# A hybrid decoder step on one Trainium2 core: the RWKV-7 recurrence's small products on the whole TensorE array, its outputs in groups of four chunks

## The chip, the cores and the metric

The kernel runs on one core of a Trainium2 chip. Five engines run side by side, each in its own fixed order: TensorE (PE, with its weight loads PEld), VectorE (DVE), ScalarE (ACT), GpSimd (POOL) and SyncE (SP, which here issues nearly all DMAs). The metric is the device time of one launch in microseconds (us), as the median of several runs.

## What is computed

One layer takes 2048 prompt tokens and 64 sample tokens (8 sequences of 8 with a paged cache of 1024 positions). After an RMSNorm one projection feeds two groups of eight heads of width 64: stick-breaking attention, and RWKV-7 time mixing. Both outputs are gated, concatenated, projected and normed. The part that the change is about is the recurrence of the second group:

```python
def _wkv_scan(r, w, k, v, a, b, s0):
    def step(S, inp):
        r_t, w_t, k_t, v_t, a_t, b_t = inp
        sa = jnp.einsum('bhvk,bhk->bhv', S, a_t)
        S = S * w_t[:, :, None, :] + sa[..., None] * b_t[:, :, None, :] + v_t[..., None] * k_t[:, :, None, :]
        return S, jnp.einsum('bhvk,bhk->bhv', S, r_t)
```

## The kernel before

The prompt goes through in four parts of 512 tokens (`hf` 0 to 3). `ORDER` (from line 347) lists for each part the projections (small letters for the RWKV group, capitals for attention), the units `U0` to `U3` of the recurrence and the attention blocks `A`. A unit is two heads over 512 tokens: sixteen units in all. Each is cut into eight chunks of 64 tokens, so there are 128 chunks.

For unit n, `rw_elem` makes decayed copies of r, k, a and b (tiles `AR`, `BK`), `rw_pairs` multiplies them into the chunk matrices `L`, and `inverse_a` with `inverse_b` inverts a triangular matrix per chunk into `NN`, on VectorE and through DRAM. `seq` then walks the chunks of unit n-1, and `rw_out` norms and gates its outputs. Two units have tiles of their own, so `AR`, `BK` and `L` of unit n+1 are those of unit n-1, and can be written only when the eight chunks of n-1 are done.

A chunk in `seq` is a chain. `fx` multiplies `L` by the state and the values (`VV`) into a bank; VectorE and ScalarE copy a half each into `XT`; `bu` multiplies by `NN`; the two engines copy the result into `VV`; `fs` (here called bs) multiplies by the transposed keys `BKT`; two VectorE instructions make the next state and write it into the next of four slots of `VV`. `fy` makes the chunk's outputs in bank `yb`, and nothing in the chain waits for it. Every second chunk the keys and values of two chunks are transposed on TensorE and copied into two slots of `BKT` and `VV`.

All products here are plain float32: each is two TensorE instructions. `fx`, bs and `fy` write 64 rows of output per head, head 0 to partitions 0 to 63 and head 1 to 64 to 127, so they use the array as two tiles of 128 rows by 64 columns; `bu` uses one such tile. The projections around them (`bank<-xh,wp`, `bank<-xl,wp`, float32r) and the transposes use the whole 128 by 128 array.

The order of every engine is fixed when the program is built. `Plan.issue` simulates the engines, and always issues the ready operation of least priority number: the recurrence's chain -0.5, the rest of a unit and `fy` 0, attention 1, projections a million, which makes them the filler of TensorE. `SWITCH` holds what the planner adds when TensorE changes from one shape of tile to another (R whole array, T transposes, A 64 columns, C, E, B other shapes); the costs written at each operation are the rest. Banks of one kind are handed out in program order (`XB` two at a time, `YB` and `MB` one).

The second stage (from line 1446) has the rest of the attention, the sample attention and the output projection. It starts when the units are finished, because it takes over their memory.

Of the kernel before, what the change touches and what calls it, by code (L numbers as in the profile page):

```python
# [9 lines left out]
F32 = mybir.dt.float32  # L10
# [3 lines left out]
AF = mybir.ActivationFunctionType  # L14
ALU = mybir.AluOpType
# [64 lines left out]
class Plan:  # L80
# [262 lines left out]
class Kern:  # L343
# [201 lines left out]
    def consts1(self, S):  # L545
# [12 lines left out]
        r = 0  # L558
# [15 lines left out]

        bo, mask, mask8 = self.bo, self.mask, self.mask8
        def masks():
# [4 lines left out]
            for m, blk in ((mask, 64), (mask8, 8)):  # L581
                nc.gpsimd.memset(m, 1.0)
                for b in range(128 // 64):
                    for a in range(2):
# [4 lines left out]
                        if blk == 8:  # L589
# [5 lines left out]
                                                    compare_op=ALU.is_ge, fill=0.0)  # L595
        op("POOL", 9500, masks, (), ["C1"])
        op("DVE", 130, lambda: nc.vector.tensor_copy(self.bor, bo), ["C1"], ["C1"])
        shT = self.shT
        bs = self.bank("X")
        for c0, n, st, sk in ((0, 8, self.units[0].AR, "AR"), (8, 8, self.units[0].BK, "BK"), (16, 1, self.units[0].L[0], "L")):  # L600
# [5 lines left out]
            op("PE", 107 * n, tr, keys, [bs.k])  # L606
        op("DVE", 210, lambda: nc.vector.tensor_copy(shT, bs.t[:, 0:136].rearrange("p (c b) -> p c b", b=8)), [bs.k], ["C1"])

# [4 lines left out]
    def const_tiles(self, S):  # L613
        nc = self.nc
        for nm, n in (("vt", 64), ("omu", 17), ("oka", 4), ("gneps", 1), ("bo", 128), ("mask", 128), ("mask8", 128), ("pv", 17), ("seqm", 8), ("sbb", 8)):
# [3 lines left out]
        self.shT = S.tile([128, 17, 8], F32, "shT").t  # L619
        self.shp = S.tile([128, 17, 9], F32, "shp").t  # L620
        self.rm = S.tile([128, 512], BF16, "rm").t
# [205 lines left out]
    def evac_rw(self, hf, ti, t0, Np, Ns, c0, ct, kind, j, bk):  # L827
# [17 lines left out]
        if Np < N:  # L845
            vs = v[:, Np:N].rearrange("p (b t) -> p b t", t=8)
            pp = ps[:, Np:N].rearrange("p (b t) -> p b t", t=8)
            self.stt(vs[:, :, 1:8], pp[:, :, 0:7], mu, vs[:, :, 1:8], ALU.mult, ALU.add, r=[bk.k], w=zk, prio=-1)
            self.stt(vs[:, :, 0], self.shT[:, ct, :], mu, vs[:, :, 0], ALU.mult, ALU.add, r=[], w=zk, prio=-1)
            self.copy(self.shp[:, ct, 0:8], pp[:, :, 7], r=[bk.k], w=[shk], prio=-1)  # L850
# [15 lines left out]
    def rwkv_tiles(self, S):  # L866
# [33 lines left out]

        self.SZ = S.ring(2, [128, 64], F32, "SZ")
        for x in self.SZ.slots:
# [245 lines left out]
    def seq(self, hf, j, c, un):  # L1148
# [37 lines left out]
        self.act(xt.t[hi, 1], bx.t[hi, 0:64], AF.Copy, r=[bx.k], w=[(xt.k, 1)], ps=True, prio=-0.5)  # L1186
        bu = self.bank("XB")
        self.pe(224, lambda: self.mm(bu.t[lo, 0:128], un.NN[:, c, :], xt.t.rearrange("p h x -> p (h x)"), True, True), r=nks + [(xt.k, 0), (xt.k, 1)], w=[bu.k], prio=-0.5, mode="A")
        self.copy(VV[lo, s_, 1, 0, :], bu.t[lo, 0:64], r=[bu.k], w=[ku + (0,)], prio=-0.5)
        self.act(VV[lo, s_, 1, 1, :], bu.t[lo, 64:128], AF.Copy, r=[bu.k], w=[ku + (1,)], ps=True, prio=-0.5)  # L1190
        kus = [ku + (0,), ku + (1,)]
        bs = self.bank("XB")
        def fs():
            for h in range(2):
                self.mm(bs.t[hr[h], 0:64], BKT[:, s_, h, :], VV[:, s_, 1, h, :], True, True)
        self.pe(215, fs, r=[kb, kv] + kus, w=[bs.k], prio=-0.5, mode="A")
        last = c == 7
        for h in range(2):
            out = self.SP[:, j, h] if last else VV[lo, sn, 0, h, :]
            self.stt(out, bs.t[hr[h], 0:64], un.WN[hr[h], c:c + 1], sw.t[hr[h]], ALU.mult, ALU.add,  # L1200
                     r=[bs.k, (sw.k, h), ("WN", U)], w=[("SP", j)] if last else [("VVS", sn)], prio=-0.5)
        if c == 0:
            self.yb = self.bank("YB")
        yb = self.yb
        y0 = 64 * c
        def fy():
            for h in range(2):
                self.mm(yb.t[hr[h], y0:y0 + 64], VV[:, s_, 1, h, :], un.L[h][:, c, 64:128], True, False)
            for h in range(2):
                st, rt = (VV[:, s_, 0, 1, :], un.RS[:, c, :]) if h else (sz.t, un.AR[:, c, 64:128])  # L1210
                self.mm(yb.t[hr[h], y0:y0 + 64], st, rt, False, True)
        self.pe(330, fy, r=kus + [kv, ks, sz.k, ("AR", U, c), ("RS", U)] + lks, w=[yb.k], mode="A")

# [638 lines left out]
```

## Time and profile before

| | us |
|---|---|
| median of 3 runs | 2099.18 (2098.11 to 2101.88) |
| the profiled execution, its time | 2096.49 |
| its span, first to last instruction | 2094.8 |
| PE busy | 1993.0 (95%) |
| DVE busy | 1607.3 (77%) |
| ACT busy | 1483.3 (71%) |

In the rows of the profile, an instruction on TensorE is named out<-moving operand, weights. `bank<-VV,L` is `fx`, `bank<-XT,NN` is `bu`, `bank<-VV,BKT` is bs, and `bank<-L,VV`, `bank<-AR,SZ`, `bank<-RS,VV` are `fy`. "128*64 128x64" means 128 rows by 64 columns of weights, 64 elements of moving operand. Starts on PE are the times at which instructions enter the array's queue; their ends are modelled and overlap with the next ones, so what a group costs is read from starts: from the start of the instruction before it to the start of the second one after it, less what those cost by themselves.

### The profile page before, as it was taken

How to read it: one execution, taken by the hardware profiler on the slowest of the kernel's cores; microseconds unless marked ns; L12 is line 12 of the kernel's file. 1: busy time of each engine (PE TensorE's matmuls, PEld its weight loads, DVE VectorE, ACT ScalarE, POOL GpSimd, SP SyncE). 2: the span in 40 equal slices, each digit the busy share in tenths (PEclk: the TensorE clock that was granted, in tenths of full speed). 3: DMA queues.
4: the chain of work that ended last, by engine and by line, in shares of the span. 5: the costliest groups of instructions: out<-in, count | busy, mean ns of one | idle time of the engine just before them, and what ended most of it. 6: DMA issues, size and time to landing. Idle time of an engine off the chain costs nothing. (4 is left out here: it accounts for less than half of the span.)

```text
span 2094.8 us, 43112 instructions
## 1 busy us (share of the span) xinstructions
PE 1993.0 (95%) x15130; PEld 1497.9 (72%) x15130; DVE 1607.3 (77%) x3770; ACT 1483.3 (71%) x3115; POOL 313.9 (15%) x854
## 2 busy tenths in 40 slices
PE   6889999999999999999999999999997999999988
PEld 5787887767777777777677777767675767676645
DVE  7798698665887888788888989889866767676732
ACT  6555454586768787877777876777687888898831
POOL 4122222110012112111221121121112000000000
PEclk9899999999999999999999999999998999999999
DMA  6977746747775675666456555555665656656454
GB/s 232 330 250 213 221 131 196 199 144 238 206 217 148 196 194 150 173 193 179 136 162 184 153 145 145 177 146 159 185 165 160 209 174 187 190 168 178 142 163 132
DMA packets 346551, 380.85 MB, mean 182 GB/s; under 512 B 127923, under 2 KB 247273, under 8 KB 346333
## 3 DMA queue, kind: packets, MB, share of 16 engines
q1 hardware_dynamic: 345948, 378.00, 61.4%
q8 instruction: 119, 1.95, 0.4%
q14 instruction: 100, 0.81, 0.1%
q0 software_dynamic: 384, 0.10, 0.0%
HBM read 268.94 MB, written 102.76 MB: 177 GB/s over the span
## 5 line engine op out<-in xcount | busy, mean ns | idle before, releaser
L63 PE MATMUL bank<-xh,wp 128*128 128x512 f32 (+2 forms) x2704 | 785.5, 364 | 10.6 <-ACT wp L63 5.8
L63 PEld LDWEIGHTS bank<-xh,wp 128*128 128x128 f32 x2704 | 476.7, 190 | 88.4 <-issue 17.5
L63 PE MATMUL bank<-xl,wp 128*128 128x512 f32 (+2 forms) x1352 | 491.4, 364 | 0.0
L63 ACT ACTIVATE T<-T 128x512 f32<-128x512 f32 (+3 forms) x608 | 345.6, 569 | 6.0
L63 DVE TENSOR_TENSOR_SCAN D<-T,car,D 128x512 f32<-128x512 f32 x180 | 230.6, 1282 | 70.0 <-ACT T L63 65.2
L63 PEld LDWEIGHTS bank<-xl,wp 128*128 128x128 f32 x1352 | 257.4, 190 | 37.2 <-issue 8.1
L63 ACT ACTIVATE At<-bank 128x512 f32<-128x512 f32 (+3 forms) x304 | 161.2, 530 | 99.6 <-PE bank L63 96.3
L63 PE MATMUL bank<-kt,qt 128*128 128x512 f32 (+3 forms) x640 | 215.9, 411 | 1.8 <-issue 1.5
L63 DVE SCALAR_TENSOR_TENSOR T<-bank,sbb,D 128x512 f32<-128x512 f32 (+3 forms) x304 | 200.9, 661 | 6.8 <-PE bank L63 0.5
L63 ACT ACTIVATE T<-bank,sbb 128x512 f32<-128x512 f32 (+3 forms) x304 | 188.5, 620 | 21.2 <-PE bank L63 14.3
L63 ACT ACTIVATE D<-bank,sbb 128x512 f32<-128x512 f32 (+3 forms) x304 | 189.4, 624 | 14.7 <-DVE T L63 10.2
L63 PE MATMUL bank<-woh,orw 128*128 128x512 f32 (+1 forms) x544 | 184.2, 406 | 8.7 <-DMA orw<-d_o 8.6
L63 PE MATMUL bank<-ident,T 128*128 128x128 f32 (+1 forms) x1156 | 174.6, 274 | 9.4 <-DVE T L63 8.2
L63 DVE TENSOR_TENSOR IMP<-IMP,IA 128x2 f32<-128x2 f32 (+30 forms) x496 | 168.3, 339 | 18.3 <-POOL IA L63 10.8
L63 PEld LDWEIGHTS bank<-ident,T 128*128 128x128 f32 (+1 forms) x1156 | 124.8, 141 | 55.3 <-DVE T L63 20.3
L63 POOL TENSOR_TENSOR SW<-VV,WC 64x64 f32<-64x64 f32 x256 | 93.1, 366 | 395.2 <-DVE VV L63 358.5
L63 PE MATMUL bank<-At,vt 128*64 128x128 f32 x1992 | 143.9, 281 | 1.6 <-ACT At L63 0.9
L63 POOL COPY car<-D 128x1 f32<-128x1 f32 x180 | 45.5, 253 | 666.9 <-DVE D L63 606.0
L63 PEld LDWEIGHTS bank<-At,vt 128*64 128x64 f32 x1992 | 108.1, 137 | 41.4 <-issue 31.9
L63 DVE TENSOR_TENSOR_SCAN D<-T,D 128x128 f32<-128x128 f32 (+3 forms) x124 | 101.0, 814 | 46.9 <-ACT T L63 40.7
L63 PEld LDWEIGHTS bank<-woh,orw 128*128 128x128 f32 (+1 forms) x544 | 99.2, 186 | 41.0 <-issue 18.8
L63 DVE TENSOR_REDUCE IMP<-IMP 128x1 f32<-128x2 f32 (+30 forms) x496 | 121.2, 244 | 7.4
(330 smaller groups left out, 3417.2 us busy)
## 6 DMA issues: line engine op xcount, KB each, us to landing
wp<-d_w SPq DMA_DIRECT2D x198, 512.0 KB
d_w<-wp SPq DMA_DIRECT2D x66, 512.0 KB
kt<-d_k SPq DMA_DIRECT2D x80, 256.0 KB
wraw<-in_w_in SPq DMA_DIRECT2D x66, 256.0 KB
qt<-d_q SPq DMA_DIRECT2D x128, 128.0 KB
orw<-d_o SPq DMA_DIRECT2D x64, 256.0 KB
vt<-out_v_prompt SPq DMA_DIRECT2D x38, 256.0 KB
IA<-d_ia SPq DMA_DIRECT2D x64, 128.0 KB
```

What stands on the lines that cost most here:

```text
L63: return f(*[x.real() if isinstance(x, Lz) else x for x in a], **{k: x.real() if isinstance(x, Lz) else x for k, x in kw.items()})
```

## The change

`fx` now writes 66 rows of output for each head, to the same partitions and to two neighbouring stretches of the bank; 66 columns of weights are over 64, so it uses the whole array. `bu` takes the weights of two neighbouring chunks, 128 columns, and the half that belongs to its chunk is read. bs becomes one product of 128 columns by 128, of which the two blocks on the diagonal are read. `fy` leaves the chunk and becomes `rw_y`, which issues the outputs of four chunks (32 instructions) after bs of the fourth, before the state that follows it; that state goes into the slot of `VV` from which the first of the four outputs reads, so it waits for `rw_y`. Copies of the state (`SZ`) that `fy` reads are kept in five tiles instead of two; two constants are merged to make room. The planner's prices of changing tiles are raised for leaving a small tile (200 in place of 15 to 90 ns), and a transpose's cost is written differently.

```diff
-    SWITCH = {("T", "T"): 81.0}
+    SWITCH = {}
     for _a in "RT":
-        for _b, _x, _y in (("A", 97.0, 55.0), ("B", 97.0, 50.0), ("C", 97.0, 90.0), ("E", 97.0, 15.0)):
-            SWITCH[_a, _b] = _x + 75.0 * (_a == "T")
-            SWITCH[_b, _a] = _y
+        for _b in "ABCE":
+            SWITCH[_a, _b], SWITCH[_b, _a] = 97.0, 200.0
...
-                SWITCH[_a, _b] = 75.0
+                SWITCH[_a, _b] = 150.0
...
-        self.pe(109 * len(terms) - 66, f, r=r, w=w, prio=prio, mode="T")
+        self.pe(109 * len(terms) + 2, f, r=r, w=w, prio=prio, mode="T")
...
-        self.SZ = S.ring(2, [128, 64], F32, "SZ")
+        self.SZ = S.ring(5, [128, 64], F32, "SZ")
...
-                self.mm(bx.t[hr[h], 0:64], un.L[h][:, c, 0:64], VV[:, s_, 0, h, :], True, True)
-        self.pe(215, fx, r=lks + [ks, kv], w=[bx.k], prio=-0.5, mode="A")
+                self.mm(bx.t[0:66, 64 * h:64 * h + 64], un.L[h][:, c, 0:66], VV[:, s_, 0, h, :], True, True)
+        self.pe(230, fx, r=lks + [ks, kv], w=[bx.k], prio=-0.5)
...
-        self.pe(224, lambda: self.mm(bu.t[lo, 0:128], un.NN[:, c, :], xt.t.rearrange("p h x -> p (h x)"), True, True), r=nks + [(xt.k, 0), (xt.k, 1)], w=[bu.k], prio=-0.5, mode="A")
+        c2, ur = min(c, 6), hr[c == 7]
+        self.pe(228, lambda: self.mm(bu.t[:, 0:128], un.NN[:, c2:c2 + 2, :].rearrange("p c i -> p (c i)"), xt.t.rearrange("p h x -> p (h x)"), True, True),
+                r=nks + [(xt.k, 0), (xt.k, 1)], w=[bu.k], prio=-0.5)
...
-                self.mm(bs.t[hr[h], 0:64], BKT[:, s_, h, :], VV[:, s_, 1, h, :], True, True)
-        self.pe(215, fs, r=[kb, kv] + kus, w=[bs.k], prio=-0.5, mode="A")
+        self.pe(228, lambda: self.mm(bs.t[:, 0:128], BKT[:, s_].rearrange("p h x -> p (h x)"), VV[:, s_, 1].rearrange("p h x -> p (h x)"), True, True),
+                r=[kb, kv] + kus, w=[bs.k], prio=-0.5)
+        if c == 0:
+            self.yb = self.bank("YB")
+        yb = self.yb
+        if c % 4 == 0:
+            self.late_y = []
+        self.late_y.append((c, s_, sz, kus + [kv, ks, sz.k, ("AR", U, c), ("RS", U)] + lks))
+        if c % 4 == 3:
+            self.rw_y(un, yb)
...
+    def rw_y(self, un, yb):
+        VV, hr = self.VV, self.HR
+        def fy(group=self.late_y):
+            for c, s_, sz, _ in group:
+                for h in range(2):
+                    self.mm(yb.t[hr[h], 64 * c:64 * c + 64], VV[:, s_, 1, h, :], un.L[h][:, c, 64:128], True, False)
+                for h in range(2):
+                    st, rt = (VV[:, s_, 0, 1, :], un.RS[:, c, :]) if h else (sz.t, un.AR[:, c, 64:128])
+                    self.mm(yb.t[hr[h], 64 * c:64 * c + 64], st, rt, False, True)
+        self.pe(962, fy, r=[k for g in self.late_y for k in g[3]], w=[yb.k], mode="A")
```

## Rows read from the trace of the kernel before

**Rows 1.** The page's first part: busy us of each engine (share of the span)

```profile
PE 1993.0 (95%) x15130; PEld 1497.9 (72%) x15130; DVE 1607.3 (77%) x3770; ACT 1483.3 (71%) x3115; POOL 313.9 (15%) x854
```

**Rows 2.** Busy us by stretch: length, then PE, PEld, DVE, ACT, POOL, clock, DMA

```profile
600.00:1000.00 400.00, 393.06 (x2946) 294.89 (x2945) 333.00 (x804) 311.74 (x649) 68.40 (x180) 1.00 0.63 178
...
1300.00:1582.00 282.00, 276.37 (x2185) 198.68 (x2180) 231.42 (x553) 214.62 (x447) 46.39 (x149) 1.00 0.58 161
...
1660.00:1990.00 330.00, 326.31 (x2457) 227.85 (x2455) 231.76 (x331) 285.77 (x570) 15.92 (x75) 0.99 0.59 174
```

**Rows 3.** Tile VV: fx and ScalarE's copies: min/median/max ns, first and last start us

```profile
L63 PE MATMUL bank<-VV,L x512: 219/222/271, 188.8 to 1576.6; 128*64 128x64 f32 x171
...
L63 ACT ACTIVATE VV<-bank x192: 197/218/598, 187.9 to 1580.8; 64x64 f32<-64x64 f32 x128, 64x512 f32<-64x512 f32 x64
```

**Rows 4.** Timeline of PE (start us, us, ...): whole-array work, no small tile between

```profile
1219.32 0.38 PE L63 MATMUL bank<-ident,BK 128*128 128x128 f32 x2
1219.54 0.38 PE L63 MATMUL bank<-ident,zv 128*128 128x128 f32 x2
1219.68 0.48 PE L63 MATMUL bank<-xl,wp 128*128 128x512 f32 x1
1219.99 0.62 PE L63 MATMUL bank<-xh,wp 128*128 128x512 f32 x2
1220.45 0.40 PE L63 MATMUL bank<-xl,wp 128*128 128x512 f32 x1
```

**Rows 5.** Timeline of PE around one bu and one fx

```profile
1032.08 0.39 PE L63 MATMUL bank<-xl,wp 128*128 128x512 f32 x1
1032.40 0.43 PE L63 MATMUL bank<-XT,NN 128*64 128x128 f32 x2
...
1033.10 0.60 PE L63 MATMUL bank<-ident,T 128*128 128x128 f32 x4
...
1035.35 0.60 PE L63 MATMUL bank<-ident,T 128*128 128x128 f32 x4
1035.88 0.34 PE L63 MATMUL bank<-VV,L 128*64 128x64 f32 x4
...
1036.48 0.63 PE L63 MATMUL bank<-xh,wp 128*128 128x512 f32 x2
```

**Rows 6.** Timeline of PE around one bs with its fy

```profile
1244.81 0.40 PE L63 MATMUL bank<-xh,wp 128*128 128x512 f32 x1
1245.14 0.34 PE L63 MATMUL bank<-VV,BKT 128*64 128x64 f32 x4
...
1245.42 0.22 PE L63 MATMUL bank<-AR,SZ 128*64 128x64 f32 x1
...
1245.48 0.22 PE L63 MATMUL bank<-AR,SZ 128*64 128x64 f32 x1
...
1245.64 0.50 PE L63 MATMUL bank<-xl,wp 128*128 128x512 f32 x1
1245.97 0.62 PE L63 MATMUL bank<-xh,wp 128*128 128x512 f32 x2
```

**Rows 7.** Timeline of PE: a plain float32 product on the whole array, 64 moving

```profile
252.69 0.33 PE L63 MATMUL bank<-splitr,bo 128*128 128x64 f32 x2
...
253.03 0.28 PE L63 MATMUL bank<-xl,wp 128*128 128x256 f32 x1
253.15 0.40 PE L63 MATMUL bank<-xh,wp 128*128 128x256 f32 x2
```

**Rows 8.** Waits of PE for other engines: us in total, times, longest us

```profile
PEld bank L63 <- ACT XT L63: 27.4, 72, 0.8
...
PEld bank L63 <- DVE VV L63: 18.7, 54, 1.3
```

**Rows 9.** Timeline of PE: the first fx of units 12 and 14

```profile
1307.41 0.73 PE L63 MATMUL bank<-VV,L 128*64 128x64 f32 x4
...
1464.15 0.39 PE L63 MATMUL bank<-VV,L 128*64 128x64 f32 x4
```

More of the change, by code (lines that the diff above doesn't have):

```diff
@@ L573, in consts1 @@
                ["vt"], ["C0"])
-        bo, mask, mask8 = self.bo, self.mask, self.mask8
+        bo, mask, mask8 = self.W3.t[:, 0:128], self.mask, self.mask8
         def masks():
@@ L595, in masks @@
                                                     compare_op=ALU.is_ge, fill=0.0)
-        op("POOL", 9500, masks, (), ["C1"])
-        op("DVE", 130, lambda: nc.vector.tensor_copy(self.bor, bo), ["C1"], ["C1"])
+        op("POOL", 9500, masks, (), ["C1", self.W3.k])
+        op("DVE", 130, lambda: nc.vector.tensor_copy(self.bor, bo), ["C1", self.W3.k], ["C1"])
         shT = self.shT
@@ L606, in consts1 @@
             op("PE", 107 * n, tr, keys, [bs.k])
-        op("DVE", 210, lambda: nc.vector.tensor_copy(shT, bs.t[:, 0:136].rearrange("p (c b) -> p c b", b=8)), [bs.k], ["C1"])
+        op("DVE", 210, lambda: nc.vector.tensor_copy(shT, bs.t[:, 0:136].rearrange("p (c b) -> p c b", b=8)), [bs.k], ["C1"] + [("shp", c) for c in range(17)])
         seqm, sbb = self.seqm, self.sbb
@@ L614, in const_tiles @@
         nc = self.nc
-        for nm, n in (("vt", 64), ("omu", 17), ("oka", 4), ("gneps", 1), ("bo", 128), ("mask", 128), ("mask8", 128), ("pv", 17), ("seqm", 8), ("sbb", 8)):
+        for nm, n in (("vt", 64), ("omu", 17), ("oka", 4), ("gneps", 1), ("mask", 128), ("mask8", 128), ("pv", 17), ("seqm", 8), ("sbb", 8)):
             setattr(self, nm, S.tile([128, n], F32, nm).t)
@@ L618, in const_tiles @@
         self.bor = S.tile([128, 128], F32R, "bor").t
-        self.shT = S.tile([128, 17, 8], F32, "shT").t
+        self.bo = self.bor.bitcast(F32)
         self.shp = S.tile([128, 17, 9], F32, "shp").t
+        self.shT = self.shp[:, :, 0:8]
         self.rm = S.tile([128, 512], BF16, "rm").t
@@ L848, in evac_rw @@
             self.stt(vs[:, :, 1:8], pp[:, :, 0:7], mu, vs[:, :, 1:8], ALU.mult, ALU.add, r=[bk.k], w=zk, prio=-1)
-            self.stt(vs[:, :, 0], self.shT[:, ct, :], mu, vs[:, :, 0], ALU.mult, ALU.add, r=[], w=zk, prio=-1)
+            self.stt(vs[:, :, 0], self.shT[:, ct, :], mu, vs[:, :, 0], ALU.mult, ALU.add, r=[shk], w=zk, prio=-1)
             self.copy(self.shp[:, ct, 0:8], pp[:, :, 7], r=[bk.k], w=[shk], prio=-1)
@@ L1181, in fx @@
             for h in range(2):
-                self.mm(bx.t[hr[h], 0:64], un.L[h][:, c, 0:64], VV[:, s_, 0, h, :], True, True)
-        self.pe(215, fx, r=lks + [ks, kv], w=[bx.k], prio=-0.5, mode="A")
+                self.mm(bx.t[0:66, 64 * h:64 * h + 64], un.L[h][:, c, 0:66], VV[:, s_, 0, h, :], True, True)
+        self.pe(230, fx, r=lks + [ks, kv], w=[bx.k], prio=-0.5)
         xt = self.XT
         self.copy(xt.t[lo, 0], bx.t[lo, 0:64], r=[bx.k], w=[(xt.k, 0)], prio=-0.5)
-        self.act(xt.t[hi, 1], bx.t[hi, 0:64], AF.Copy, r=[bx.k], w=[(xt.k, 1)], ps=True, prio=-0.5)
+        self.act(xt.t[hi, 1], bx.t[lo, 64:128], AF.Copy, r=[bx.k], w=[(xt.k, 1)], ps=True, prio=-0.5)
         bu = self.bank("XB")
-        self.pe(224, lambda: self.mm(bu.t[lo, 0:128], un.NN[:, c, :], xt.t.rearrange("p h x -> p (h x)"), True, True), r=nks + [(xt.k, 0), (xt.k, 1)], w=[bu.k], prio=-0.5, mode="A")
-        self.copy(VV[lo, s_, 1, 0, :], bu.t[lo, 0:64], r=[bu.k], w=[ku + (0,)], prio=-0.5)
-        self.act(VV[lo, s_, 1, 1, :], bu.t[lo, 64:128], AF.Copy, r=[bu.k], w=[ku + (1,)], ps=True, prio=-0.5)
+        c2, ur = min(c, 6), hr[c == 7]
+        self.pe(228, lambda: self.mm(bu.t[:, 0:128], un.NN[:, c2:c2 + 2, :].rearrange("p c i -> p (c i)"), xt.t.rearrange("p h x -> p (h x)"), True, True),
+                r=nks + [(xt.k, 0), (xt.k, 1)], w=[bu.k], prio=-0.5)
+        self.copy(VV[lo, s_, 1, 0, :], bu.t[ur, 0:64], r=[bu.k], w=[ku + (0,)], prio=-0.5)
+        self.act(VV[lo, s_, 1, 1, :], bu.t[ur, 64:128], AF.Copy, r=[bu.k], w=[ku + (1,)], ps=True, prio=-0.5)
         kus = [ku + (0,), ku + (1,)]
         bs = self.bank("XB")
-        def fs():
-            for h in range(2):
-                self.mm(bs.t[hr[h], 0:64], BKT[:, s_, h, :], VV[:, s_, 1, h, :], True, True)
-        self.pe(215, fs, r=[kb, kv] + kus, w=[bs.k], prio=-0.5, mode="A")
+        self.pe(228, lambda: self.mm(bs.t[:, 0:128], BKT[:, s_].rearrange("p h x -> p (h x)"), VV[:, s_, 1].rearrange("p h x -> p (h x)"), True, True),
[8 more added lines that the diff above has]
+            self.rw_y(un, yb)
         last = c == 7
@@ L1199, in seq @@
             out = self.SP[:, j, h] if last else VV[lo, sn, 0, h, :]
-            self.stt(out, bs.t[hr[h], 0:64], un.WN[hr[h], c:c + 1], sw.t[hr[h]], ALU.mult, ALU.add,
+            self.stt(out, bs.t[hr[h], 64 * h:64 * h + 64], un.WN[hr[h], c:c + 1], sw.t[hr[h]], ALU.mult, ALU.add,
                      r=[bs.k, (sw.k, h), ("WN", U)], w=[("SP", j)] if last else [("VVS", sn)], prio=-0.5)
[L1202 to L1212, printed above, removed]
+    def rw_y(self, un, yb):
[8 more added lines that the diff above has]
+        self.pe(962, fy, r=[k for g in self.late_y for k in g[3]], w=[yb.k], mode="A")
     def rw_out(self, hf, j, t0, N, c0, un, yb):
```

## The prediction

> **What bounds the kernel now.** I read the shares of busy time first: TensorE is busy for 95% of the span, VectorE 77%, ScalarE 71% [rows 1]. An average hides stages, so the stretches came next: from 600 to 1000 and from 1300 to 1582 us, where the recurrence runs, TensorE is busy 98% and VectorE 82 to 83%; from 1660 to 1990 us, after it, TensorE 99% and ScalarE 87% [rows 2]. Projections, at the last priority, fill whatever the recurrence leaves, so a microsecond of TensorE saved there should shorten the run as long as there are projections to bring forward. The waits add a warning: TensorE reaches bu before its input 72 times out of 128, and a product that waits for what VectorE writes into `VV` 54 times [rows 8]. In 126 of the 384 steps of the chain TensorE is there first; the chain is the second limit, close behind. Last, the timeline around single products, where "busy" misleads: array work and changes of tile are both counted. There I read starts.
>
> **What a visit to the small tiles costs.** With nothing but whole-array work around, a 512-column projection takes 0.23 us from start to start (1219.99 to 1220.45 is two), and four transposes 0.44 (1219.32 to 1219.99 less one projection), 0.11 each [rows 4]. Around bu, 1032.08 to 1033.10 is 1.02; less two projections it costs 0.56. Around fx, 1035.35 to 1036.48 is 1.13; less four transposes and a projection, 0.46 [rows 5]. bs with its fy: 1244.81 to 1245.97, less two, 0.70; inside it a pair of instructions, one for each half of the array, comes every 0.06 [rows 6]. The array work in these is two pairs (0.12), two instructions of 0.11 (0.22), and six pairs (0.36): what is left is 0.34 each time. So a visit costs 0.34 us for going in and out, and a chunk makes three: 1.72 us, of which 1.02 is the change of tile. Of the 384 visits between the first and the last of [rows 3], I count 54 in the timeline that stand in one run with attention's 64-column products; those pay no 0.34 of their own.
>
> **The change, part by part.** *fx on the whole array.* Four instructions of 64 moving elements. The row for such a product shows two at 0.34 less 0.12 for the projection behind them, 0.11 each with 128 columns of weights [rows 7], though the pair pitch shows 0.06 of array work [rows 6]: there the weight load sets the pace. fx has 66 columns, about half the load. Bounds: 0.24 (all at 0.06) and 0.44 (all at 0.11). I take three at 0.06 and the last at 0.11, since the next instruction's load is a full one: 0.29. The 66 columns are nearest to the 64 of [rows 6].
>
> *bu and bs.* Two instructions each of 128 moving elements. Lower end 0.22, the transposes' pace [rows 4]. Upper end 0.32: if 0.05 of the load stays exposed at each, as it does in [rows 7]. I take 0.22, because at 128 elements the array work (0.11) is as long as the load's 0.11.
>
> The skill has a rule against this part: the Trainium skill, TensorEngine Tiling (Array Packing), Theoretical Speedup, gives up to two times for splitting the array when a side is 64 or less, and the change gives that up for fx and bs. [rows 6] bear it out for array work alone. By that rule only, fx and bs would each cost about 0.1 us more.
>
> *fy in groups.* Sixteen pairs at 0.06 and one visit: 0.96 + 0.34 = 1.30 for four chunks, 0.33 a chunk.
>
> *Sum.* After: 0.29 + 0.22 + 0.22 + 0.33 = 1.06 a chunk against 1.72, so 0.66, times 128: 84 us. The 54 shared visits had no 0.34 to lose: less 18. That is 66 us of TensorE. With the upper ends of fx, bu and bs a chunk takes 1.41: 40 less 18, 22 us. With fx at 0.24, 73.
>
> *The new wait.* The state after the fourth chunk now waits for the group, 1.30 us, and so do the copies that put the next values into the slots that the group reads (one ScalarE copy of 0.6, the longest of [rows 3]): up to 1.9 us later, once in a unit's walk; behind the eighth chunk `rw_out` starts 1.0 us later. Queued behind the waiting state on VectorE are softmax steps of attention, and behind the copy on ScalarE its exponentials. Against it, the chain's own steps no longer pay the way into a small tile, 0.09 us of the 0.34 (1035.35 and 0.44 of transposes, to 1035.88 [rows 5]), three times in each of eight chunks: 2.2 us. For the chain I book nothing. If the group's wait finds VectorE or ScalarE in a long instruction twice, it is 1 to 2 us worse per unit.
>
> *Prices and order.* The old prices put a visit at 97 in and 55 out where 340 is seen, so the plan was ahead of TensorE. The new order cannot be read from this trace. What it can win is bounded by TensorE's waits of [rows 8], 46 us; I take 0, with 10 us either way. Tile `SZ`, the merged constants and the later taking of bank `YB` move no instruction on the path: nothing.
>
> **How much of the 66 us arrives.** Half of the chunks belong to the first eight units, which run up to about 1000 us with projections still to come; TensorE idles 2% there [rows 2]. Of their 33 us I let 85% arrive, 28. From unit 8 on the units follow a loop: walk of n, then the elementwise work of n+2 (its tiles are n's), its pairs, inverse and walk; unit 12 to unit 14 takes 156.7 us [rows 9]. The loop holds little of the saved time, so TensorE runs ahead of it and in part finds no projection left; attention then fills some, and what it does early is off the stretch from 1660 us, where TensorE is 99% busy. I let half arrive, 17 (33 to 0 are the ends). Together 45 us.
>
> **The sum.** The profiled execution took 2096.5 us (span 2094.8, 1.7 around it); less 45, 2051.5. The median of the runs shown is 2.7 above that execution, so 2054 on the scale of the medians.
>
> **The rivals.**
>
> *All of it arrives and the order gets better* (66 to 80 us: 2019 to 2033). For it: TensorE at 98 to 99% on both sides of 1600 us. Against: the just-in-time steps of [rows 8].
>
> *The loop of the units takes it back.* The second half gives nothing and the first half little, or the full loads stay exposed (22 us in all): 8 to 28 us, 2071 to 2091. For it: [rows 9], and the 126 waits of [rows 8]. Against: TensorE at 98% in the same stretch, which says that the two limits are level, not that the loop leads.
>
> *The change does not do what it says.* Whole-array products behind float32r ones might still pay the way in and out. Then nothing moves, within 4 us of 2099. [rows 7] speak against it: there two such instructions cost 0.22 with all that is lost behind them, 0.12 less than the way in and out alone.
>
> *Slower: the group of outputs lands on the loop.* The fourth state waits 1.3 us for the group and the next values 0.6 more, on a queue where a copy meets one of its own length in front: 2.5 us per unit. It decides from the point at which the loop, and not TensorE, sets the pace; with eight units on the loop 20 us, and if no saving arrives the time is 2119.
>
> *Slower: the array work, with the change of tile hidden before.* Where TensorE waits for a step's input anyway, the way into the tile costs nothing, and its removal gains nothing; fx still grows from 0.12 to 0.29 and bs from 0.12 to 0.22, 0.27 a chunk, 35 us. For it: the 126 waits of [rows 8]. Against: the other 258 steps did not wait, and the way out is paid by the projection behind. It decides if nearly all steps waited; then 2134. The rule of the skill (TensorEngine Tiling (Array Packing), Theoretical Speedup) points this way.
>
> **How the numbers follow.** Forecast, 30 to 62 us off (2037 to 2069): 0.55. All of it, 2019 to 2037: 0.15. The loop takes it back, 2069 to 2091: 0.14. Nothing, within 0.2% (about what a measurement of this kernel can tell from no change): 0.04. Group on the loop, slower: 0.09. Array work, slower: 0.03. That is 0.84 faster, 0.04 same, 0.12 slower. The range leaves out the two slow cases, the null, and the outermost of the gain: 2022 to 2092.
>
> **What would show it.** In the profile after: fx, bu and bs as 128-row products of over 64 columns, with a projection's pace of 0.23 right behind them; fx at 0.24 to 0.44 by starts, bu at 0.22; 32 groups of outputs of about 1.3 us; weight loads idle for "issue" a good deal less. TensorE's busy time should fall by about as much as the span. If the loop takes it back, TensorE's idle time between 1000 and 1582 us grows by 15 us or more and unit 12 to 14 still takes about 156 us; if the group is on the loop, the step from chunk 3 to chunk 4 is 2 us longer than the others. I am wrong in the sum if fx comes out at 0.44 or bu at 0.33, and wrong in the share if TensorE's busy time falls by 66 us and the time by less than 30.

## The result, and the profile after

| | before | after |
|---|---|---|
| median of 5 runs, side by side, us | 2098.14 (2094.32 to 2101.88) | 2077.54 (2073.68 to 2083.43) |
| ratio, 95% interval | 1 | 0.9899 [0.9877, 0.9920] |
| profiled execution, us | 2096.49 | 2078.69 |
| its span, us | 2094.8 | 2077.0 |

The change makes the kernel 20.6 us faster (16 to 26 by the interval), with the list order that the planner drew for it; what another order does to such a number is asked under the experiments. The forecast was 45 us.

Busy time of the engines after, beside [rows 1]:

```profile
PE 1974.6 (95%) x14874; PEld 1528.8 (74%) x14874; DVE 1610.9 (78%) x3770; ACT 1475.5 (71%) x3115; POOL 318.9 (15%) x857
```

TensorE's busy time fell by 18 us, about as much as the span, and not by 66. The stretches of [rows 2], in the same columns:

```profile
600.00:1000.00 400.00, 391.44 (x2920) 303.54 (x2919) 331.73 (x817) 305.58 (x643) 67.91 (x182) 0.98 0.63 178
...
1300.00:1582.00 282.00, 265.49 (x2103) 204.74 (x2103) 233.04 (x556) 213.18 (x448) 51.81 (x147) 0.97 0.60 171
...
1660.00:1990.00 330.00, 327.25 (x2478) 226.53 (x2477) 234.99 (x328) 284.77 (x566) 15.37 (x73) 1.00 0.59 173
```

Of these, only the stretch from 1300 to 1582 us got idler on TensorE by more than 2 us: 265.5 us busy in place of 276.4. The work itself came out as priced. One fx, one bu, and one bs with its group of outputs, in the timeline of TensorE after (start us, us, what):

```profile
1015.75 0.62 PE L63 MATMUL bank<-xh,wp 128*128 128x512 f32 x2
1016.21 0.40 PE L63 MATMUL bank<-VV,L 128*66 128x64 f32 x4
1016.42 0.48 PE L63 MATMUL bank<-xl,wp 128*128 128x512 f32 x1
1016.74 0.63 PE L63 MATMUL bank<-xh,wp 128*128 128x512 f32 x2
...
1092.81 0.38 PE L63 MATMUL bank<-XT,NN 128*128 128x128 f32 x2
1093.03 0.60 PE L63 MATMUL bank<-ident,T 128*128 128x128 f32 x4
...
1245.85 0.42 PE L63 MATMUL bank<-VV,BKT 128*128 128x128 f32 x2
1246.19 0.34 PE L63 MATMUL bank<-L,VV 128*64 128x64 f32 x4
...
1247.12 0.22 PE L63 MATMUL bank<-RS,VV 128*64 128x64 f32 x1
1247.28 0.50 PE L63 MATMUL bank<-xl,wp 128*128 128x512 f32 x1
1247.61 0.39 PE L63 MATMUL bank<-xh,wp 128*128 128x512 f32 x1
```

fx: 1015.75 to 1016.74 less three projections of 0.23 is 0.30 (0.46 in [rows 5]). bu: 1092.81 to 1093.03, 0.22 (0.56). bs with the group: 1245.85 to 1247.61 less one projection, 1.53; less 0.22 for bs, 1.31 for four chunks. The prediction had 0.29, 0.22, 0.22 and 1.30 (the 0.22 of bs is taken from bu here; the table below has it for bs alone).

These are clean visits. Many are not. I took every visit that has whole-array work on both sides, by the starts around it, in both traces (81 to 101 visits of a kind before, 78 to 105 after; 14 groups):

| us | before: median, mean | after: lower quarter, median, mean |
|---|---|---|
| fx | 0.47, 0.56 | 0.29, 0.29, 0.39 |
| bu | 0.57, 0.64 | 0.23, 0.40, 0.45 |
| bs with fy; after, bs alone | 0.69, 0.71 | 0.22, 0.33, 0.38 |
| bs with a group of four | | 1.51, 1.57, 1.61 |

By the means, in the kernel before a chunk took 0.56 + 0.64 + 0.71, 1.90 before rounding, so 0.18 over the clean 1.72. After it takes 0.39 + 0.45 + 0.38 + (1.61 - 0.38)/4 = 1.53, 0.47 over the clean 1.06. So a chunk saved 0.37 and not 0.66: 47 us over 128 chunks, less the 18 of the shared visits (the prediction's figure), 29 us.

Most of the rest became waits inside the same visits. To see it, I split the visits of the table by when they begin: with their input, which is at most 0.15 us after the end of the last write to it (for bu the copies into `XT`, for bs and fx the copies and the state in `VV`), or later.

| | before: begin with their input | after: begin with their input | after: mean of these, of the others, us |
|---|---|---|---|
| bu | 43 of 97 | 71 of 105 | 0.54, 0.27 |
| bs | 17 of 81 | 51 of 78 | 0.46, 0.23 |
| fx | 26 of 101 | 35 of 102 | 0.41, 0.38 |

A bu or bs whose input has been there for a while costs 0.27 or 0.23, near its clean price; one that begins with its input costs twice that, and there are many more of these than before. For fx the split explains little; what its 0.10 over the clean price is, stays open. Not all of this shows as idle time of TensorE, because the modelled end of the product in front covers a part of such a wait: in the rows of a bu below, a projection that takes 0.23 counts as busy for 0.50.

TensorE's waits after, as in [rows 8], and under them two of before that do not stand there:

```profile
PEld bank L63 <- DVE T L63: 43.1, 89, 3.7
PEld bank L63 <- ACT XT L63: 31.4, 72, 2.1
PEld bank L63 <- ACT VV L63: 28.9, 73, 1.2
...
PEld bank L63 <- DVE VV L63: 10.2, 22, 1.6
```

```profile
PEld bank L63 <- DVE T L63: 24.5, 51, 2.7
...
PEld bank L63 <- ACT VV L63: 10.0, 28, 0.9
```

Waits for what ScalarE copies into `VV` went from 28 to 73, waits for what VectorE writes there from 54 to 22; the two together from 28.7 to 39.1 us. For bs alone, the view of its tile `BKT` has what TensorE and its weight loads waited for ScalarE's copy, before and after (us, times):

```profile
  ACT VV L63: 7.2, 17
```

```profile
  ACT VV L63: 28.2, 73
```

The waits for `XT`, on which bu depends, went from 27.4 to 31.4 us. Those for `T`, a tile that attention's softmax steps write on VectorE, grew by 18.6 us; no run says why. Here is a bu after that waits for `XT`, with weight loads and ScalarE's copy:

```profile
1022.91 0.50 PE L63 MATMUL bank<-xl,wp 128*128 128x512 f32 x1
1023.16 0.21 ACT L63 ACTIVATE XT<-bank 64x64 f32<-64x64 f32 x1
1023.43 0.30 PEld L63 LDWEIGHTS bank<-XT,NN 128*128 128x128 f32 x2 [0.34 <-ACT XT L63]
1023.43 0.49 PE L63 MATMUL bank<-XT,NN 128*128 128x128 f32 x2
```

ScalarE's copy of `XT` ends at 1023.37, and bu starts at 1023.43, 0.52 after the projection, which by itself takes 0.23.

Where the saved time went is seen in the last projection and the last bs. A tile's rows give minimum, median and maximum in ns, then the first and the last start. Before:

```profile
L63 PE MATMUL bank<-xh,wp x2704: 274/389/792, 16.5 to 1576.1; 128*128 128x512 f32 x110, 128*128 128x256 f32 x49, 128*128 128x320 f32 x35
...
L63 PE MATMUL bank<-VV,BKT x512: 219/222/369, 193.4 to 1581.4; 128*64 128x64 f32 x171
```

After:

```profile
L63 PE MATMUL bank<-xh,wp x2704: 274/389/795, 15.2 to 1545.1; 128*128 128x512 f32 x110, 128*128 128x256 f32 x47, 128*128 128x320 f32 x37
...
L63 PE MATMUL bank<-VV,BKT x256: 270/275/582, 191.6 to 1585.7; 128*128 128x128 f32 x128
```

The projections end 31 us earlier, which agrees with the 29 us from the visits. The walk of the last unit ends 4 us later. None of the lead was there in the first half: the projections' products by stretch (length, PE busy and count, PEld busy and count, and so on), before and then after, stand at 2903 by 990 us in both, and the lead of 41 is made from 990 to 1300 us.

```profile
0.00:990.00 990.00, 608.34 (x2903) 456.54 (x2903) 23.57 (x33) 41.04 (x66) 45.05 (x33) 0.99 0.67 200
990.00:1300.00 310.00, 172.09 (x648) 111.41 (x648) 0.00 (x0) 0.00 (x0) 0.00 (x0) 1.00 0.56 156
```

```profile
0.00:990.00 990.00, 612.69 (x2903) 461.56 (x2903) 22.58 (x33) 41.26 (x66) 45.26 (x33) 0.97 0.67 201
990.00:1300.00 310.00, 179.24 (x689) 118.94 (x688) 0.00 (x0) 0.00 (x0) 0.00 (x0) 0.99 0.57 159
```

The first fx of units 12 and 14, as in [rows 9]:

```profile
1312.93 0.59 PE L63 MATMUL bank<-VV,L 128*66 128x64 f32 x4 [0.81 <-DMA L<-AR]
...
1469.26 0.63 PE L63 MATMUL bank<-VV,L 128*66 128x64 f32 x4 [1.39 <-DMA L<-AR]
```

They stand 156.3 us apart, 156.7 before, and start 5 us later than before. TensorE brought its filler forward, then ran out of it before the walk was over (length, PE, PEld, DVE, ACT, POOL, clock, DMA):

```profile
1485.00:1520.00 35.00, 34.00 (x270) 25.85 (x269) 33.01 (x100) 24.95 (x63) 8.57 (x24) 1.00 0.60 176
1520.00:1560.00 40.00, 35.04 (x288) 27.57 (x286) 24.02 (x41) 32.86 (x67) 4.66 (x17) 0.91 0.46 123
1560.00:1600.00 40.00, 32.15 (x242) 22.75 (x241) 31.24 (x55) 32.20 (x66) 11.35 (x31) 0.88 0.60 177
```

What reached the end shows in attention: its last product of queries and keys starts at 1968 us and not 1994, and the span is 18 us shorter.

```profile
L63 PE MATMUL bank<-kt,qt x640: 222/397/776, 394.7 to 1994.3; 128*128 128x512 f32 x112, 128*128 128x128 f32 x16, 128*128 128x256 f32 x16, 128*128 128x384 f32 x16
```

```profile
L63 PE MATMUL bank<-kt,qt x640: 220/397/795, 394.9 to 1967.8; 128*128 128x512 f32 x112, 128*128 128x128 f32 x16, 128*128 128x256 f32 x16, 128*128 128x384 f32 x16
```

### The profile page after: what moved, and what is told of

Its sections match the earlier page's. It is cut to its first block, busy times and chain, and to the rows that moved or that the text cites. A ratio compares the mean times of both kernels' runs of the same rounds, so it can differ in the third digit from the quotient of the medians.

```text
span 2077.0 us, 42593 instructions
## 1 busy us (share of the span) xinstructions
PE 1974.6 (95%) x14874; PEld 1528.8 (74%) x14874; DVE 1610.9 (78%) x3770; ACT 1475.5 (71%) x3115; POOL 318.9 (15%) x857
## 4 chain that ended last, share of the span: by engine, by line
PE 32%; DVE 10%; ACT 9%; DMA 4%; issue 2%; SPq 2%; POOL 0%; DVEq 0%; POOLq 0%; ACTq 0%
PE bank L63 32%; ACT T L63 3%; DVE D L63 3%; DVE IMP L63 2%; SPq L63 2%; DVE T L63 2%; ACT D L63 1%; DVE VV L63 1%; ACT At L63 1%; ACT VV L63 1%; DMA L<-AR 1%; DMA IMP<-d_im 0%; DMA NN<-d_im 0%; ACT tmprn L63 0%; ACT IA L63 0%
## 5 line engine op out<-in xcount | busy, mean ns | idle before, releaser
L63 PEld LDWEIGHTS bank<-xh,wp 128*128 128x128 f32 x2704 | 482.0, 193 | 68.2 <-issue 7.5
```

The costliest lines, as they stand in the source:

```text
L63: return f(*[x.real() if isinstance(x, Lz) else x for x in a], **{k: x.real() if isinstance(x, Lz) else x for k, x in kw.items()})
```

## The experiments

In all of them the ratio is to the kernel before, run beside it on the same chip; a number of us is the difference of the medians.

### First questions: the group, the prices, the amount of work

**Smaller groups of outputs.** The groups are 0 to 2, 3 to 5 and 6 to 7, so no state waits for a group.

```diff
-        if c % 4 == 0:
+        if c % 3 == 0:
...
-        if c % 4 == 3:
+        if c % 3 == 2 or c == 7:
             self.rw_y(un, yb)
...
-        self.pe(962, fy, r=[k for g in self.late_y for k in g[3]], w=[yb.k], mode="A")
+        self.pe(233 * len(self.late_y) + 30, fy, r=[k for g in self.late_y for k in g[3]], w=[yb.k], mode="A")
```

> The changed kernel with the outputs in groups of chunks 0 to 2, 3 to 5 and 6 to 7 instead of 0 to 3 and 4 to 7: the slot that a group reads first is overwritten one chunk later, so no state waits for the outputs; one more visit to the small tiles per unit (16 times 0.34 us). Theory GROUP: 20 to 35 us faster than the changed kernel (2043 to 2058), the step from chunk 3 to chunk 4 back from 7.3 to about 6 us. Theory LOOP: the loop gets 1 to 2 us per unit shorter, 5 to 15 us faster than the changed kernel (2063 to 2073). Rival PRICES: no change beyond 5 us.

Measured: 2081.02 us, ratio 0.9927 [0.9901, 0.9952], 16 us faster than before; the changed kernel is 21. The step from the first fx of chunk 3 to that of chunk 4 went back from 7.3 us on average to 5.5, which is what it was in the kernel before, and the time did not fall. That is PRICES (within 5 us of the changed kernel); GROUP and LOOP fall. The group's wait costs the chain 1.8 us per unit and the end nothing that can be seen in this one pair of list orders.

**Old and new prices apart.**

```diff
-        for _b in "ABCE":
-            SWITCH[_a, _b], SWITCH[_b, _a] = 97.0, 200.0
+        for _b, _x, _y in (("A", 97.0, 55.0), ("B", 97.0, 50.0), ("C", 97.0, 90.0), ("E", 97.0, 15.0)):
+            SWITCH[_a, _b] = _x + 75.0 * (_a == "T")
+            SWITCH[_b, _a] = _y
...
-        self.pe(109 * len(terms) + 2, f, r=r, w=w, prio=prio, mode="T")
+        self.pe(109 * len(terms) - 66, f, r=r, w=w, prio=prio, mode="T")
```

> The changed kernel with the planner's old prices of tile changes and of transposes; the instructions are the same, only their order differs. Rival PRICES (the dearer prices make a worse order and cost what is missing): 20 to 45 us faster than the changed kernel. LOOP and GROUP: within 10 us of the changed kernel, either way.

Measured, the changed kernel with the old prices: 2062.48 us, ratio 0.9825 [0.9797, 0.9852], 35 us faster than before and 15 faster than the changed kernel, between what PRICES and the other two asked for. The same edit the other way round, the new prices alone on the kernel before:

> The kernel before with the new prices alone. Rival PRICES: 15 us or more slower than before. Rival PRICES-HELP (the truer prices are what made the changed kernel faster, and the products brought nothing): about 20 us faster than before. LOOP and GROUP: within 8 us of before.

Measured: 2145.53 us, ratio 1.0224 [1.0197, 1.0251], 48 us slower, as PRICES says. So the plan is worth as much as the products; whether by the prices or by chance is asked below.

**Less work.** Two of 24 products in each tile of the projections are gone, and the planner knows of it:

```diff
                     for i, (a, b, nm) in enumerate(((wh, xh, "xh"), (wh, xl, "xl"), (wl, xh, "xh"))):
+                        if (k, i) in ((2, 1), (5, 1)):
+                            continue
```

> The kernel before, with two of the 24 products of every projection left out (169 projection tiles, 338 products of 0.12 to 0.23 us, about 65 us of TensorE; so the projections are not the reference's), and nothing else changed: a saving of the size that the change was to bring, without its waits, its tiles and its prices. Theory LOOP (in the second half the loop of the units, walk of n to elementwise work, inverse and walk of n+2, sets the pace, so that only a part of any TensorE saving arrives): 15 to 30 us faster than before, unit 12 to unit 14 still 150 to 160 us apart. Rival GROUP (the change's own wait of the fourth state for the outputs took the rest) and rival PRICES (the new order took it): 50 to 65 us faster, since neither is in this kernel.

Measured: 2105.83 us, ratio 1.0035 [1.0019, 1.0052], 8 us slower with some 65 us less for TensorE; LOOP and both rivals had it faster. The logarithm pass left out in every fourth softmax block of prompt attention:

```diff
-        self.act(t, t, AF.Ln, r=[T.k], w=[T.k], bias=1.0, tab=LNE)
+        self.nch = getattr(self, "nch", 0) + 1
+        if rings[0] is not self.Tr or self.nch % 4:
+            self.act(t, t, AF.Ln, r=[T.k], w=[T.k], bias=1.0, tab=LNE)
```

> The kernel before, with the pass for the logarithm left out in every fourth block of the prompt's attention (80 instructions of about 0.57 us on ScalarE, 45 us; the attention weights of those blocks are not the reference's). PACE: 20 to 45 us faster than before, the last attention block 20 to 45 us earlier. LOOP (the loop of the units sets the end): within 8 us of before, since the units' chain has not changed.

Measured: 2111.34 us, ratio 1.0052 [1.0036, 1.0068], 9 us slower with some 45 us less for ScalarE, which neither theory had.

**More work.** Three more products in each tile of the projections, about 100 us of TensorE, in the kernel before and in the changed one:

```diff
+                        for _ in range(3 if k == i == 0 else 0):
+                            self.pe(N / 2.4 + 16, lambda o=o, a=a, b=b: self.mm(o, a[0].t[:, 0, :], b, True, True), r=..., w=[bk.k], prio=PL)
```

> The kernel before, with three extra products ahead of each of the 169 projection tiles (507 of 0.12 to 0.23 us, about 100 us of TensorE; they are overwritten, and nothing else is added). Theory PACE (the run ends some 100 us after the last attention block, and attention advances at the pace of ScalarE, VectorE and its own chain; a saving on TensorE becomes waits of TensorE): the added work fills TensorE's small slack and the rest shows: 60 to 100 us slower than before. Rival TENSOR (TensorE's work sets the time): 95 to 105 us slower.

> The changed kernel with the same 507 extra products. PACE: what the change saved on TensorE stands in it as slack, so the extra work costs 40 us less than in the kernel before, and the two kernels with extra work are 50 to 70 us apart (they are 21 apart without it). TENSOR: the extra work costs both the same 100 us, and they stay 20 to 25 us apart.

Measured: 2177.37 us, ratio 1.0352 [1.0331, 1.0374], and 2156.55 us, ratio 1.0256 [1.0232, 1.0279]. About three quarters of the added TensorE work reach the end, in both kernels, and the two still stand 21 us apart, as TENSOR has it; PACE's slack in the changed kernel did not show. Each is one list order, so a reserve of the size of the scatter below is not excluded.

**Attention ahead of the units,** in the changed kernel with old prices, to give TensorE other filler during the walk:

```diff
-    PA = 1.0
+    PA = -0.2
```

> The changed kernel with the old prices (35 us faster than before) and attention's priority raised from 1 to -0.2, ahead of all of a unit but the chain of the recurrence. PACE: the last attention block comes earlier, and the units later; 0 to 30 us faster than with the old prices alone until the end of the units takes over. LOOP: the units' loop gets longer, 20 us or more slower than with the old prices alone.

Measured: 2136.76 us, ratio 1.0173 [1.0154, 1.0193], by the ratios 73 us slower than the same kernel with the units first, as LOOP says. The units have to lead.

In these runs adding to TensorE costs and taking from it gains nothing. Since every such edit also makes the planner draw another list order, the next runs kept the order.

### With the order of the kernel before kept

In these, the planner sees the old operations at the old costs, every engine gets the list of before, and only what is emitted differs.

**Less TensorE, same order.**

```diff
-                            self.mm(o, a[k // 4].t[:, k % 4, :], b, 3 * k + i == 0, 3 * k + i == 23)
+                            if (k, i) not in ((2, 1), (5, 1)):
+                                self.mm(o, a[k // 4].t[:, k % 4, :], b, 3 * k + i == 0, 3 * k + i == 23)
```

> The kernel before with its planned order kept, instruction for instruction, except that two of the 24 products in each tile of the projections are not emitted, while the planner still counts them: 338 products fewer, about 65 us of TensorE by the same edit's earlier run, in which the planner knew of it and made another order (that one was 8 us slower than before). Part of the projections' sum is left out. ORDER (the list order that the planner makes is drawn anew by any change of its numbers, the order of before is a good draw, and a saving of TensorE shows when the order stays): 40 to 65 us faster than before. SLACK (TensorE's time is not what the end hangs on; time taken from it turns into waits whatever the order): 0 to 20 us faster.

Measured: 2090.36 us, ratio 0.9961 [0.9943, 0.9980]. It is 7 us faster: SLACK, and ORDER in the form stated there falls. TensorE's busy time fell by 37 us and not by 65. The page's parts on busy time and on the chain that ended last (shares of the span):

```profile
PE 1956.4 (94%) x14792; PEld 1446.2 (69%) x14792; DVE 1604.8 (77%) x3770; ACT 1481.2 (71%) x3115; POOL 314.6 (15%) x854
```

```profile
PE 48%; DVE 23%; DMA 11%; ACT 11%; issue 4%; SPq 2%; POOL 0%; DVEq 0%; ACTq 0%; POOLq 0%
```

This chain could be followed over the whole span. TensorE is busy 94% of the time, and less than half of the way to the end lies on it. That share is no constant of the kernel: in the run below with half of the inverse the followed chain has 73% on TensorE.

**fx and bu on the whole array, same order.** bs and fy stay on their tiles.

```diff
-                self.mm(bx.t[hr[h], 0:64], un.L[h][:, c, 0:64], VV[:, s_, 0, h, :], True, True)
+                self.mm(bx.t[0:66, 64 * h:64 * h + 64], un.L[h][:, c, 0:66], VV[:, s_, 0, h, :], True, True)
...
-        self.pe(224, lambda: self.mm(bu.t[lo, 0:128], un.NN[:, c, :], xt...
+        self.pe(224, lambda: self.mm(bu.t[:, 0:128], un.NN[:, c2:c2 + 2, :].rearrange("p c i -> p (c i)"), xt...
...
```

> The kernel before with its planned order kept, instruction for instruction, and the products fx and bu emitted on the whole array as in the changed kernel; bs and fy stay on tiles and the planner keeps all its old numbers. By the durations in the changed kernel fx goes from 0.46 to 0.29 us and bu from 0.56 to 0.22, 0.51 x 128 chunks = 65 us, less about 10 for tile changes that other tiled products now pay alone: 55 us of TensorE. ORDER: 35 to 55 us faster than before, so more than the whole change gives (21). SLACK: 0 to 20 us faster.

Measured: 2086.76 us, ratio 0.9948 [0.9930, 0.9966]. It is 11 us faster where the instructions alone are worth some 55: SLACK. Because the lists are the same, each visit can be laid beside itself, from the instruction before it to the one after it: the fx visits are 9 us shorter in all and the bu visits 12, and 41 of 127 and 62 of 128 did not get shorter by even 0.05 us. Measured to the second instruction after it, as the prediction priced a visit, the sums are 11 and 15. One bu, in the kernel before:

```profile
1347.01 0.22 ACT L63 ACTIVATE XT<-bank 64x64 f32<-64x64 f32 x1
...
1347.05 0.42 PE L63 MATMUL bank<-kt,qt 128*128 128x128 f32 x2
...
1347.40 0.43 PE L63 MATMUL bank<-XT,NN 128*64 128x128 f32 x2
...
1347.80 0.48 PE L63 MATMUL bank<-xl,wp 128*128 128x512 f32 x1
```

and the same bu with the whole array:

```profile
1339.38 0.22 ACT L63 ACTIVATE XT<-bank 64x64 f32<-64x64 f32 x1
...
1339.42 0.42 PE L63 MATMUL bank<-kt,qt 128*128 128x128 f32 x2
...
1339.68 0.46 PE L63 MATMUL bank<-XT,NN 128*128 128x128 f32 x2
...
1340.00 0.47 PE L63 MATMUL bank<-xl,wp 128*128 128x512 f32 x1
```

From the products before bu to the projection behind it: 0.75 before, 0.58 after, 0.17 saved of 0.34. ScalarE's copy of `XT` ends at 1339.60, so bu can hardly start earlier than 1339.68.

**Half of the inverse, same order.** Every second step on VectorE left out of the triangular inverse:

```diff
             self.dve(70 + 1.04 * m * i, lambda ...: nc.vector.tensor_reduce(out=IM.t[:, 0:m, t:t + 1], ...
+            if t % 2:
+                for o in self.P.ops[-2:]:
+                    o.fn = lambda: None
```

> The kernel before with its planned order kept; in the inverse of each unit every second of the 31 steps on VectorE (a product and its sum) is not emitted, half of a part of the computation left out: about 145 us of VectorE less (half of 168.3 and 121.2 us), and a serial piece that stands between a unit's pairs and its walk shortened by about 9 us in each of 16 units. WALK (the loop of the units sets the end of the walk, and through it the end): 40 us faster or more. LEVEL (the lists of TensorE, VectorE and ScalarE and the recurrence's steps stand level, so that none gives much alone): 5 to 25 us faster.

Measured: 2081.41 us, ratio 0.9913 [0.9886, 0.9941], 19 us faster. LEVEL; the loop of the units is not the one limit, since a piece of about 9 us (as planned) was taken out of each of sixteen units. VectorE's busy time fell by 116 us, and unit 12 to unit 14 still took 154.6 us (1297.73 to 1452.35), 156.7 before.

**Less ScalarE, same order.** The logarithm of every fourth block not emitted.

```diff
         self.act(t, t, AF.Ln, r=[T.k], w=[T.k], bias=1.0, tab=LNE)
+        self.nch = getattr(self, "nch", 0) + 1
+        if rings[0] is self.Tr and self.nch % 4 == 0:
+            self.P.ops[-1].fn = lambda: None
```

> The kernel before with its planned order kept; the logarithm pass is not emitted in every fourth softmax block of prompt attention (left out of the computation): about 45 us of ScalarE less. LEVEL and WALK: 0 to 12 us faster. If ScalarE were the bound: 30 us or more.

Measured: 2098.05 us, ratio 0.9990 [0.9972, 1.0008]: 3 us, no difference that can be told, as LEVEL and WALK have it.

**All three together, same order.** The three edits above in one kernel.

> The kernel before with its planned order kept and all three left out together: 338 products of the projections (65 us of TensorE), half of the inverse's steps (145 us of VectorE), and every fourth logarithm pass of prompt attention (45 us of ScalarE). LEVEL: 50 us faster or more, clearly over the sum of the three single gains. WALK: about what the inverse alone gives, within 10 us. If the gains simply add: their sum.

Measured: 2056.72 us, ratio 0.9799 [0.9774, 0.9824], 44 us faster; by the ratios 42, where the single ones give 8 + 18 + 2 = 28. The sum is exceeded by half, so what one engine gives up another does keep, as LEVEL says; but the 50 us that LEVEL asked for are missed, and a part simply adds. None of the three forms holds as stated.

### How far list orders scatter

Steps in the planner that mean nothing, in four kernels, to see how much of any difference is the draw of the order:

```diff
-        self.pe(109 * len(terms) - 66, f, r=r, w=w, prio=prio, mode="T")
+        self.pe(109 * len(terms) - 64, f, r=r, w=w, prio=prio, mode="T")
```

and, in the second one of before,

```diff
-    LAG = {("PE", "ACT"): 197.0, ...
+    LAG = {("PE", "ACT"): 198.0, ...
```

> The kernel before with one number of the planner changed that means nothing: a group of transposes is planned 2 ns dearer. The same operations; the planner's list order comes out different. ORDER: 10 to 50 us away from before, likelier slower. SLACK: within 6 us of before, since nothing real has changed.

> The kernel before with another meaningless step: the planner's delay from TensorE to ScalarE is 198 in place of 197 ns. The same operations in another list order. ORDER, with the first step's 16 us slower: between 5 us faster and 30 us slower than before, likelier slower, since the order of before has been the fastest of its kind so far. SLACK: within 6 us.

> The changed kernel with the same meaningless step of 2 ns in the planned price of a group of transposes. The same operations in another list order. ORDER: 10 to 45 us away from the changed kernel, either way. SLACK: within 6 us of it.

> The changed kernel with the planner's old prices of tile changes, and a group of transposes planned 2 ns dearer than before, a number that means nothing. PRICES-HELP (the old prices make the better plan for the changed kernel): within 8 us of the same kernel without the step of 2 ns, so 27 to 43 us faster than before. ORDER (its 15 us over the changed kernel were the scatter between orders): 8 us or more slower than without the step, 10 to 27 us faster than before.

> The kernel before with the planner's new prices of tile changes alone, and a group of transposes planned 2 ns dearer still. PRICES (visits priced at 297 in place of about 150 ns make a worse plan for a kernel with 384 of them): 30 to 60 us slower than before, like the run without the step (47 slower). ORDER (that run was one unlucky order): 0 to 30 us slower than before.

| kernel | us against before, by the ratio | after a meaningless step |
|---|---|---|
| before | 0 | +16 [+10, +21]; +2 [-1, +5] |
| before, new prices | +47 [+41, +53] | +51 [+46, +56] |
| changed kernel | -21 [-26, -17] | -12 [-18, -7] |
| changed kernel, old prices | -37 [-43, -31] | -11 [-15, -7] |

The same operations in another order differ by up to 26 us. The 48 us that the new prices cost the kernel before came back with a second order: they are the prices' own. The 15 us that the old prices seemed to give the changed kernel did not come back, so PRICES-HELP is not shown there; 2062 us is the fastest version here, but partly a lucky draw.

This bears on the result itself: its 21 us are no larger than the scatter. What speaks for a gain beyond the draw is that all four orders of the changed kernel (-11 to -37) lie below all three of before with its own prices (0 to +16). How much of the 21 belongs to the products and how much to the draw is not shown.

## Why the prediction was wrong

**What held.** The price of a visit and the new prices of the instructions: 0.30, 0.22, 0.22 and 1.31 in clean visits, to 0.01 of the sum; the two signs of a wrong sum that the prediction names, fx at 0.44 or bu at 0.33 in such a visit, did not come. The group: 1.8 us more in the step from chunk 3 to chunk 4 (5.5 to 7.3), predicted as up to 1.9, and off the path, as far as the one run with smaller groups can tell. The rule of the Trainium skill, TensorEngine Tiling (Array Packing), Theoretical Speedup, gives up to two times for splitting the array when a dimension is 64 or less. The clean visits here do not bear it out: fx takes 0.30 whole and 0.46 split.

**The step that failed first: the sum of what is removed.** The prediction took the clean price off each of 384 visits, less 18 us, and booked nothing for the chain. It had the row against this in hand: [rows 8], 126 visits in which TensorE already stood waiting. It read them as a warning, let the other 258 stand as free to shrink, and did not ask how much slack those had. In the trace before, 186 of the 279 visits of the table begin within what they were to save (0.17, 0.34 and 0.48 us) of the moment at which their input was ready, taken as 0.06 us after its last write. With visits that much shorter TensorE arrives early at the next product too, and what it saved it waits: the mean over the clean price grew from 0.18 to 0.47 us a chunk. That turns 66 us of TensorE into 29, and the projections' end, 31 us earlier, is a second count of it. The run with the order kept shows the step by itself: fx and bu shorter by 21 us, or 26 with the instruction behind, where 55 were in the instructions. The rival "the array work, with the change of tile hidden before" named this mechanism, but as a case for nearly all visits or none.

**The second: the share that arrives.** Its total came out, 20.6 of 29 or 0.71, where the forecast has 45 of 66 or 0.68; that is luck, since its parts did not. 85% of the first half was to arrive because projections were still to come. But by 990 us TensorE had started as many of their products as before, 2903, and unit 8 starts at 989 us and not 993: of the first half at most those 5 us had arrived, and the lead is made in the second. And the share is no fixed thing: with the order kept, 7 of 65 us of removed projections arrived, and 11 of the 21 to 26 of fx and bu. "The loop of the units takes it back" is the rival in whose range the time lies (2071 to 2091); unit 12 to 14 kept its 156 us, as it asked. TensorE's idle time from 1000 to 1582 us grew by 11 us (568.64 us busy before, 557.31 after), where it asked for 15. The name is too narrow, though: shortening the loop itself, by half of the inverse, gave 19 us, and no single engine relieved in that way (37 us of busy time on TensorE, 116 on VectorE, 39 on ScalarE) gave more. The reading that fits is that TensorE, VectorE, ScalarE and the chain between them stand about level, while a share was forecast for one of them as if it led; the sum of all three, 44 us where 50 were asked, supports it in part.

**The third: "prices and order, nothing, with 10 either way".** Two orders of the same changed kernel lie 9 us apart, with old prices 26; three orders of before up to 16. And the new prices have a cost of their own: 48 and 51 us on the kernel before, in two orders. How much of that the changed kernel pays, where 32 of the 384 visits are left, is open: against the old prices it is 15 us in one pair of orders and none in the other.

**A rival that no run settles: the clock.** The mean granted clock was 0.978 in the five runs of the changed kernel and 0.984 in the kernel before. Over 2077 us that is, by my estimate, at most 12 us of full clock, half of what is missing from the forecast. It does not explain the visits: the means of the table stay within 0.01 when the visits in stretches at 1.2 GHz are left out, and the run with fx and bu alone has 0.984 and lost the saving all the same. It may have a part in the share that arrived: 0.97 by 990 us, 0.99 before. Against a large part: the smaller groups, at 0.983, were no faster.

**What stays open.** Why the new prices make a worse plan was not tried. Nor was the changed kernel as a whole run in the order of before: its grouped outputs have no place in that list. And the removal of 65 us of TensorE that gave 7 is not traced to one successor; the chain after it names four (TensorE, VectorE, DMA, ScalarE).

## What to carry to other kernels

Before taking a clean price off each visit, look at how long the visit's input had been ready: where a product follows its producer by less than the saving, the difference can turn into a wait, at this product or at the next. A busy share of 95% did not mean here that work removed pays (7 of 65 us with the order kept), though work added did cost (three quarters of an estimated 100 us, in one order each). Where a planner draws the order, keep the order to measure an edit, or measure it over several orders, since steps of 2 ns moved this kernel by up to 26 us.

## What the runs showed of the hardware

A plain float32 product with 66 columns of weights on the whole array came every 0.06 us at 64 moving elements (by the starts of the four in fx; in the sum, four in 0.30 less 0.11 for the last), where 128 columns took 0.11 [rows 7]. From 600 to 1590 us the granted clock is 2.4 GHz throughout in the profile of the kernel before; after, seven stretches in it are at 1.2 GHz, 34 us in all. In the rows above, TensorE is busy 35.04 of 40 and 32.15 of 40 us where the mean clock is 0.91 and 0.88, and 34.00 of 35 where it is 1.00. That the waits of the shorter visits brought this on is not shown: the kernel before, in the order after the first meaningless step, has 20.5 us at 1.2 GHz between 600 and 1590 us with the old visits.
